# Hybrid DeltaNet, gMLP and MLP block: the operands of the MLP made ahead into device memory, one pool of 2 KB tiles, units in pairs

## The chip, the cores and the metric

The kernel runs on one core of a Trainium2 chip. The metric is the time of one execution on the device in microseconds (us), lower is better. The engines are named as in the profile: PE (TensorE, matrix products), DVE (VectorE), ACT (ScalarE), POOL (GpSimd) and SP (SyncE, which issues nearly all DMAs here). On-chip memory has 128 partitions; PSUM is the memory that PE writes to, in 8 banks of 128x512 fp32.

## What is computed

One trunk layer over 128 prompt tokens and 2048 latent tokens of width 1024, all in fp32:

```python
def block(x, s0, mod, ...):
    sh1, sc1, ga1, sh2, sc2, ga2 = mod
    h = rmsnorm(x, norm_mix_l) * (1.0 + sc1) + sh1
    o, s_new = mixer(h, s0, ...)      # projections, conv, DeltaNet scans both ways, gMLP, output projection
    x = x + ga1 * o
    h = rmsnorm(x, norm_ffn_l) * (1.0 + sc2) + sh2
    x = x + ga2 * (jnp.square(jax.nn.relu(h @ w_ff1_l)) @ w_ff2_l)
    return x, s_new
```

`w_ff1` is 1024 x 4096 and `w_ff2` 4096 x 1024. A last RMSNorm follows. The change concerns the last two lines: h, and the two products of the MLP.

## The kernel before

The 2176 tokens are 17 tiles of 128: tile 0 is the prompt, 1 to 16 are latent. Four phases follow each other; their instructions are written in an order of steps with due times, and a scheduler then sets the order on each engine.

**Projections** (to about 455 us): combined input projection and convolution; results go to device memory.

**Attention** (about 455 to 1283 us): the DeltaNet scan forward over the tiles, then backward (from about 924 us, tile 16 first), with gMLP and the output projection among the scan's steps. Each backward unit takes one tile of 128 tokens: loads, a preparation, a serial scan on PE, DVE and ACT, then the output projection. `h2_steps` (L801) belongs to a finished tile: it normalises the token rows, transposes and modulates them, and stores the result, transposed, in device memory (`h2_d`, profile name `h_d`). It runs for tiles 16 to 9 among the backward units (`spread(... h2_steps ...)`, behind L1275) and for tiles 8 to 0 during the first half of the MLP's first phase (`later`, L1548). A list of windows (`WINDOWS`) gives each kind of step its place relative to its unit.

**MLP up** (about 1283 to 2041 us): relu(h w_ff1) squared. fp32 accuracy is had from three fp32r matmuls per product, with operands split into a high and a low half (`mm3`, L215; L219 to L221). The product is done by a scheme with seven block products in place of eight: tokens are taken in two groups of 8 tiles (group 0: tiles 9 to 16; group 1: tiles 1 to 8), and a **unit** (`unit`, L1449) is one group by 256 of the 4096 hidden columns. It makes products 1, 5, 6, 7, 3, 2, 4 in this order, each 12 matmuls of 128x512 in PSUM, with sums and squares on DVE and ACT after most, and stores z (and two sums of z, `s1_d`, `s2_d`) to device memory. A unit's operands:

- the moving side (`hop`): seven operands per group, 16 KB per partition each. `token_steps` (L1356) makes them at the start of each group: 28 loads of 128x512 from `h2_d` (`hraw`), differences of these on DVE (L1377, L1383, L1388, L1395), a cast to the high half on ACT (L1369), and a subtraction for the low half on DVE (L1370). For group 0 these steps are interleaved with the first unit's weights; for group 1 they stand behind group 0's last unit.
- the stationary side (`wH`, `wL`): `weight_steps` (L1400) loads a unit's 1 MB of w_ff1 by two DMAs of 512 KB and makes the seven weight operands (`split4`, L1347: cast at L1352, subtraction at L1353), one unit ahead.

Group 1's units also do the prompt tile with 48 matmuls of 128x128 (`single`, L1523).

**MLP down** (about 2041 us to the end): z w_ff2 by the same scheme, now with seven products outside and the token pairs inside. For each of the products 1, 5, 6, 7, 3, 4, 2 the 16 moving tiles T (`t_load`, `t_build`, L1612 to L1621: load of a part of w_ff2 or of a sum of its parts in `t13_d`, `t2_d`, `t4_d`; ACT cast L1619, DVE L1620) are made during the product before; the sums are made by `sums_load` and `sums` (L1627 to L1650). The stationary tiles come from z: `s_load`, `s_build` (L1670 to L1686), with loads five steps and halves three steps ahead (`AHEAD = 3`). Results are kept in `ya`, `yb` and finished by `final` (L1704). Modulation rows for the second gate are computed among products 6 and 7 (`mods`, L1755).

**Pools.** Each phase has its own: `wp` (48 tiles of 128x512) and `stage` for projections and attention, closed by `wst.close()`; `f1w` (14 tiles `t`, 18 `hl`), `f1h`, `f1p` for MLP up; `f2w` (5 `traw`, 6 `sraw`, 20 `T`, 12 `s`), `f2p` for MLP down. A tile of a new pool waits until what used its place before is done.

```python
todo = [(gi, jp) for gi in range(2) for jp in range(NP)]
ops, steps = token_steps(9 * P)
w, prep = weight_steps(0, False)
interleave(steps, prep)
for n, (gi, jp) in enumerate(todo):
    main = unit(jp, c0, w, ops)
    nw, prep = weight_steps(todo[n + 1][1], ...)
    interleave(*[x for x in (main, prep, extra) if x])
    if n == NP - 1:
        ops, steps = token_steps(P)
        for st in steps:
            st()
```

Of the kernel before, what the change touches and what calls it, by code (L numbers as in the profile page):

```python
# [17 lines left out]
P = 128  # L18
# [34 lines left out]
FT = 14  # L53
FW = 18
# [7 lines left out]
def hybrid_step(  # L62
# [36 lines left out]
    h2_d = dp.tile([P, KT, NTOK], F32, name="h2_d")  # L99
# [6 lines left out]
    z_d = dp.tile([NT, P, 2, NK, P], F32, name="z_d")  # L106
    s1_d = dp.tile([8, P, NK, P], F32, name="s1_d")
    s2_d = dp.tile([8, P, NK, P], F32, name="s2_d")
    t13_d = dp.tile([NK, P, 2, 512], F32, name="t13_d")
    t2_d = dp.tile([NK, P, 512], F32, name="t2_d")  # L110
    t4_d = dp.tile([NK, P, 512], F32, name="t4_d")
# [54 lines left out]
    smp = ctx.enter_context(tc.tile_pool(name="small", bufs=4, reuse_waits="tile"))  # L166
    wst = ctx.enter_context(ExitStack())
# [11 lines left out]
    wp = wst.enter_context(tc.tile_pool(name="wp", bufs=48, reuse_waits="tile"))  # L179
    sp = wst.enter_context(tc.tile_pool(name="stage", bufs=NS))  # L180
# [620 lines left out]
    def h2_steps(t, psum, tmp, wide=w512):  # L801
# [17 lines left out]
        def trans2(half):  # L819
            def f():  # L820
                ps = psum()
                ev = tmp()
                for i in range(4):
                    T.transpose(ps[:, i * P : (i + 1) * P], u["x"][half][:, i * P : (i + 1) * P], ident)
                for i in range(4):
# [3 lines left out]
                store(out=h2_d[:, half * 4 : half * 4 + 4, t * P : (t + 1) * P],  # L829
                      in_=ev.rearrange("p (k d) -> p k d", k=4))  # L830
            return f

        return [norm2, trans2(0), trans2(1)]
# [4 lines left out]

    with ExitStack() as ph:
        pp = ph.enter_context(tc.tile_pool(name="prep", bufs=1, reuse_waits="tile"))  # L840
        hp = ph.enter_context(tc.tile_pool(name="hp", bufs=8, reuse_waits="tile"))
        dl = ph.enter_context(tc.tile_pool(name="scan", bufs=1, reuse_waits="tile"))
# [22 lines left out]
        def load_rows(src, t, d):  # L865
            gb = q32("gb", 3, pp)
            rows = src[t * 8 + d * 4 : t * 8 + d * 4 + 4, :].rearrange("a b -> (a b)").unsqueeze(0)
            load(out=gb.rearrange("p h d -> p (h d)"), in_=rows.to_broadcast([P, 512]))
            return gb
# [5 lines left out]
        def unit(t, d):  # L875
# [11 lines left out]
            def prep_loads():  # L887
# [3 lines left out]
                u["QK"] = q32("QK", 3, pp)  # L891
# [353 lines left out]

        events = []
# [25 lines left out]
        for i, u in enumerate(units):  # L1272
# [4 lines left out]
            for j, st in enumerate(u["prep"]):  # L1277
                at(i - w[0] + (j + 0.5) * (w[0] - w[1]) / n, st, "chain")
# [3 lines left out]
            if i >= NT:  # L1282
# [4 lines left out]
                if u["t"] > 8:  # L1287
                    spread(i + p3[8], i + p3[9], h2_steps(u["t"], pj, fraw), "fill")
# [20 lines left out]
        spread(p2[6], p2[7], [lambda n=n, k=k: load_wo(n, k) for n in range(2) for k in range(KT)], None)  # L1309
        hist = []  # L1310

        def emit(f, kind, lag):
# [6 lines left out]
            if pe and kind == "chain":  # L1319
# [17 lines left out]
    with ExitStack() as ph:  # L1337
        fw = ph.enter_context(tc.tile_pool(name="f1w", bufs=1, reuse_waits="tile"))
        fh = ph.enter_context(tc.tile_pool(name="f1h", bufs=1, reuse_waits="tile"))
        psq = ph.enter_context(tc.tile_pool(name="f1p", bufs=1, space=PSUM, reuse_waits="tile"))  # L1340

        def bank():
            return psq.tile([P, 512], F32, tag="f", name="f", bufs=8)

        def t512(name="t"):
            return fw.tile([P, 512], F32, tag="t", name=name, bufs=FT)

        def split4(src):

            h = fw.tile([P, 4, P], F32R, tag="hl", name="wH", bufs=FW)  # L1350
            lo = fw.tile([P, 4, P], F32R, tag="hl", name="wL", bufs=FW)
            A.copy(h, src)  # L1352
            V.tensor_tensor(out=lo, in0=src, in1=f32(h), op=ALU.subtract)  # L1353
            return h, lo

        def token_steps(c0):  # L1356

            ops, b, tt = {}, {}, {}

            def raw(n, kp):  # L1360
                kh, th = divmod(n, 2)
                r = t512("hraw")
                load(out=r, in_=h2_d[:, kh * 4 + kp, c0 + th * 512 : c0 + th * 512 + 512])
                return r

            def put(i, kp, src):
                if kp == 0:
                    ops[i] = fh.tile([P, 4, 2, 512], F32R, tag="hop", name="hop", bufs=7)
                A.copy(ops[i][:, kp, 0, :], src)  # L1369
                V.tensor_tensor(out=ops[i][:, kp, 1, :], in0=src, in1=f32(ops[i])[:, kp, 0, :], op=ALU.subtract)  # L1370

            def p1(kp):
                put(1, kp, raw(0, kp))

            def p5(kp):
                x, y = raw(1, kp), raw(0, kp)
                V.tensor_tensor(out=x, in0=x, in1=y, op=ALU.subtract)  # L1377
                tt[kp] = x
                put(5, kp, x)

            def p6(kp):
                x = raw(3, kp)
                V.tensor_tensor(out=tt[kp], in0=x, in1=tt[kp], op=ALU.subtract)  # L1383
                put(6, kp, tt[kp])

            def p7(kp):
                x, y = raw(3, kp), raw(1, kp)
                V.tensor_tensor(out=y, in0=x, in1=y, op=ALU.subtract)  # L1388
                put(7, kp, y)
                put(3, kp, x)  # L1390

            def p2(kp):
                x = raw(2, kp)
                put(2, kp, x)
# [5 lines left out]
        def weight_steps(jp, extra):  # L1400
# [10 lines left out]
            def a(i, j):  # L1411
                return r[j][:, :, i * P : i * P + P]
# [468 lines left out]
```

## Time and profile before

| what | us |
|---|---|
| median of 3 runs | 2753.39 |
| lowest and highest of them | 2744.67, 2754.87 |
| the profiled execution | 2746.23 |
| its span, first to last instruction | 2744.5 |
| PE busy in the span | 2637.6 |
| DVE, ACT, POOL busy | 1870.7, 1261.2, 232.0 |
| bytes moved by DMA | 541.04 MB, mean 197 GB/s |

How to read what follows. A row of the windows gives the stretch in us, its length, then for PE, PEld (weight loads), DVE, ACT and POOL the busy time with the number of instructions, then the granted clock of PE (1.00 is full), the mean busy share of the 16 DMA engines, and GB/s. A row of the groups gives line, engine, operation, out<-in, shapes and count, then busy us and mean ns, then the idle time of the engine before these instructions with what ended it. A row of the waits gives engine, line, what ended the wait, then us in total, number of times, and the longest. A row of the timeline gives start, duration, instruction, and in brackets the idle time before it. A row of the chain of waits gives start, duration and what ran. A matmul's recorded duration is longer than its share of PE's time, since matmuls overlap; the pace is read from the distance of starts.

### The profile page before, as it was taken

What the parts mean: (1) busy time and instruction counts of PE and PEld (TensorE: products, weight loads), DVE (VectorE), ACT (ScalarE), POOL (GpSimd) and SP (SyncE); (2) the same over time, 40 slices, a digit from 0 to 9 for tenths busy, and PEclk for the clock granted to TensorE, in tenths of its full rate; (3) what the DMA queues carried; (4) which work ended last, traced back from release to release, by engine and by line L of the source; (5) the groups of instructions that cost most, each with busy time, mean ns of one, the idle gap of its engine ahead of it and who ended that gap; (6) DMA issues with size and microseconds to landing.
All of it is one profiled execution on the core that took longest, in us unless ns stands there. A gap on an engine that the chain in (4) does not pass through costs nothing.

```text
span 2744.5 us, 45073 instructions
## 1 busy us (share of the span) xinstructions
PE 2637.6 (96%) x15698; PEld 2196.1 (80%) x15698; DVE 1870.7 (68%) x3911; ACT 1261.2 (46%) x3094; POOL 232.0 (8%) x448
## 2 busy tenths in 40 slices
PE   8999998999999899998899989999989999899998
PEld 4999997888887777786688877888877878688887
DVE  5867656867777887775877678566645546775675
ACT  4655555555555666642544434333323332332442
POOL 3112113111111111100000000000000000000000
PEclk9999998999999999998999999999999999999999
DMA  8867549545455667743556564443349888766664
GB/s 293 278 196 220 179 141 285 179 151 161 156 157 182 209 208 219 226 154 128 167 163 179 161 189 150 117 121 112 111 146 402 313 286 282 248 222 213 219 218 143
DMA packets 489130, 541.04 MB, mean 197 GB/s; under 512 B 32748, under 2 KB 327068, under 8 KB 488902
## 3 DMA queue, kind: packets, MB, share of 16 engines
q1 hardware_dynamic: 487894, 536.33, 61.2%
q8 instruction: 123, 2.02, 0.3%
q10 hardware_dynamic: 1008, 1.84, 0.2%
q14 instruction: 105, 0.86, 0.1%
HBM read 383.46 MB, written 154.57 MB: 196 GB/s over the span
## 4 chain that ended last, share of the span: by engine, by line
PE 78%; DMA 10%; DVE 8%; ACT 2%; issue 1%; SPq 1%; POOL 0%; DVEq 0%; POOLq 0%; ACTq 0%
PE f L220 8%; PE f L219 7%; PE f L221 7%; PE yps L220 7%; PE yps L219 7%; PE yps L221 7%; PE pj L219 6%; PE pj L221 6%; PE pj L220 6%; PE pd L885 2%; DMA qT<-qT_d 2%; PE pm L219 1%; PE pm L221 1%; PE pm L220 1%; DMA raw<-in_w_mod_dram 1%
## 5 line engine op out<-in xcount | busy, mean ns | idle before, releaser
L219 PE MATMUL yps<-T,zH 128*128 128x512 f32 x960 | 373.6, 394 | 15.9 <-ACT T L1619 15.7
L220 PE MATMUL yps<-T,zH 128*128 128x512 f32 x960 | 377.0, 393 | 5.4 <-DVE T L1620 5.3
L219 PE MATMUL f<-hop,wH 128*128 128x512 f32 x896 | 355.9, 399 | 22.4 <-ACT hop L1369 9.6
L221 PE MATMUL yps<-T,zL 128*128 128x512 f32 x960 | 375.4, 392 | 0.0
L220 PE MATMUL f<-hop,wH 128*128 128x512 f32 x896 | 354.6, 396 | 11.1 <-DVE hop L1370 10.9
L221 PE MATMUL f<-hop,wL 128*128 128x512 f32 x896 | 353.1, 395 | 0.0
L1684 ACT CAST zH<-sraw 128x512 fp32r<-128x512 f32 x240 | 147.2, 622 | 287.6 <-PE yps L220 223.4
L219 PEld LDWEIGHTS yps<-T,zH 128*128 128x128 f32 x960 | 181.9, 190 | 59.7 <-ACT T L1619 18.9
L219 PEld LDWEIGHTS f<-hop,wH 128*128 128x128 f32 x896 | 170.8, 191 | 62.8 <-ACT hop L1369 13.2
L220 PEld LDWEIGHTS yps<-T,zH 128*128 128x128 f32 x960 | 181.8, 189 | 48.4 <-DVE T L1620 10.4
L1685 DVE TENSOR_TENSOR zL<-sraw,zH 128x512 fp32r<-128x512 f32 x240 | 163.2, 687 | 80.4 <-ACT zH L1684 71.4
L220 PEld LDWEIGHTS f<-hop,wH 128*128 128x128 f32 x896 | 170.5, 190 | 53.3 <-DVE hop L1370 19.7
L221 PEld LDWEIGHTS yps<-T,zL 128*128 128x128 f32 x960 | 181.8, 189 | 37.3
L221 PEld LDWEIGHTS f<-hop,wL 128*128 128x128 f32 x896 | 170.5, 190 | 35.1 <-DVE wL L1353 0.2
L219 PE MATMUL pj<-kH,wH 128*128 128x386 f32 (+2 forms) x568 | 190.5, 338 | 0.3 <-DVE kH L468 0.3
L221 PE MATMUL pj<-kH,wL 128*128 128x386 f32 (+2 forms) x568 | 190.3, 335 | 0.0
L220 PE MATMUL pj<-kL,wH 128*128 128x386 f32 (+2 forms) x568 | 189.4, 334 | 0.0
L177 POOL TENSOR_TENSOR r<-rsq,nhalf 128x1 f32<-128x1 f32 (+1 forms) x38 | 26.7, 701 | 1593.6 <-DVE rsq L176 1593.6
L1352 ACT CAST wH<-raw 128x512 fp32r<-128x512 f32 x112 | 69.5, 622 | 139.8 <-PE f L220 138.9
L518 DVE SCALAR_TENSOR_TENSOR cv<-pj,vec,cv 128x384 f32<-128x384 f32 (+2 forms) x164 | 87.4, 540 | 58.4 <-ACT cv L515 57.2
L1352 ACT CAST wH<-s 128x512 fp32r<-128x512 f32 x96 | 59.9, 624 | 132.1 <-PE f L220 112.4
L1353 DVE TENSOR_TENSOR wL<-raw,wH 128x512 fp32r<-128x512 f32 x112 | 77.2, 691 | 52.0 <-ACT wH L1352 40.8
(402 smaller groups left out, 6185.9 us busy)
## 6 DMA issues: line engine op xcount, KB each, us to landing
sraw<-z_d SPq DMA_DIRECT2D x209, 256.0 KB
raw<-in_w_ff_dram SPq DMA_DIRECT2D x64, 512.0 KB
z_d<-c SPq DMA_DIRECT2D x96, 256.0 KB
sraw<-s_d SPq DMA_DIRECT2D x96, 256.0 KB
raw<-in_w_mod_dram SPq DMA_DIRECT2D x80, 256.0 KB
s_d<-s SPq DMA_DIRECT2D x64, 256.0 KB
traw<-t_d SPq DMA_DIRECT2D x64, 256.0 KB
hraw<-h_d SPq DMA_DIRECT2D x56, 256.0 KB
```

The source lines that it names most:

```text
L177: G.tensor_tensor(out=out, in0=t[:np_, :n], in1=nhalf[:np_, :n], op=ALU.pow)
L219: T.matmul(ps, lh, rh, start=first and i == 0, stop=False, skip_group_check=more)
L220: T.matmul(ps, lh, rl, start=False, stop=False, skip_group_check=more)
L221: T.matmul(ps, ll, rh, start=False, stop=last and i == n - 1, skip_group_check=more)
L518: V.scalar_tensor_tensor(out=cv[:, o : o + m], in0=ps[:, s + sh : s + sh + m], scalar=convw[:, w, j : j + 1], in1=cv[:, o : o + m], op0=AL ...
L885: T.matmul(p[:, h, :], lhs[:, h, :], rhs[:, h, :], start=True, stop=True)
L1352: A.copy(h, src)
L1353: V.tensor_tensor(out=lo, in0=src, in1=f32(h), op=ALU.subtract)
L1684: A.copy(h, r)
L1685: V.tensor_tensor(out=lo, in0=r, in1=f32(h), op=ALU.subtract)
```

## The change

- **Operands made ahead.** For tiles 9 to 12 and 1 to 4, `h2_steps` no longer stores `h2_d`. It loads the stored `h2_d` of the partner tile (`t + 4`), makes the part of each of the seven operands that belongs to the two tiles, both halves, and stores it to `hop_d[group, operand]` in device memory (`put`). For tiles 9 to 12 these steps run in attention, over the stretch of one unit behind the tile's own steps; for tiles 4 to 1 they run in group 0 of MLP up (`later`). `hop_next` loads one operand, 2 MB, with two DMAs; operands 1 and 5 of group 0 are loaded after the last preparation of a scan unit, the other five at the start of the MLP, those of group 1 after the products of group 0's last unit. `token_steps` is gone.
- **One pool.** `wp`, now 49 tiles of 2 KB per partition, stays open to the end and serves weights, raw tiles, z, results and rows in all phases. Seven tiles of 16 KB (`hopA` 2, `hopB` 5) hold the operands of MLP up, then the T tiles and the kept results x and q of MLP down. `hopA` takes the place of the pool `prep`, closed early (`swap_right`).
- **Units in pairs where operands change.** Units 0 and 1, 14 and 15 of each group alternate product by product, so that each moving operand serves two products in a row. Weights are made 6 products ahead (`LEAD`), their loads issued 10 products ahead. The weights' loads are four DMAs of 256 KB in place of two of 512 KB. The prompt tile's matmuls are spread over the unit's products.
- **First tiles of MLP down** (T of product 1 and the first z tiles) are made during the last 16 products of MLP up.
- **Device tensors split**: `h2_d` per tile, `z_d` in 5, `s1_d` and `s2_d` in 2, the sums of w_ff2 one tensor per product and part (`t_d`).

Per engine, the orders of the two kernels have as many PE instructions before as after; the DMA issues on SP go from 2028 to 2235.

The core of the diff:

```diff
-                store(out=h2_d[:, half * 4 : half * 4 + 4, t * P : (t + 1) * P],
-                      in_=ev.rearrange("p (k d) -> p k d", k=4))
+                if t in h2_d:
+                    store(out=h2_d[t][:, half * 4 : half * 4 + 4, :], in_=ev.rearrange("p (k d) -> p k d", k=4))
+                else:
+                    u[half] = ev
...
+        def partner():
+            u["y"] = [wide("y"), wide("y")]
+            for half, y in enumerate(u["y"]):
+                load(out=y.rearrange("p (k d) -> p k d", k=4), in_=h2_d[t + 4][:, half * 4 : half * 4 + 4, :])
+
+        def put(o, src):
+            dst = hop_d[t <= 8, o][:, :, :, (t - 1) % 4 * P : (t - 1) % 4 * P + P]
+            h = wp.tile([P, 512], F32R, tag="w", name="opH")
+            lo = wp.tile([P, 512], F32R, tag="w", name="opL")
+            A.copy(h, src)
+            V.tensor_tensor(out=lo, in0=src, in1=f32(h), op=ALU.subtract)
+            for i, part in enumerate((h, lo)):
+                store(out=dst[:, :, i, :], in_=f32(part).rearrange("p (k d) -> p k d", k=4))
+
+        def plain():
+            put(1, u[0])
+            put(2, u[1])
+        def third():
+            put(3, u["y"][1])
+            d = wide("d")
+            sub(u["y"][1], u["y"][0], d)
+            put(7, d)
+        def fifth():
+            sub(u["y"][0], u[0])
+            put(5, u["y"][0])
+        def sixth():
+            sub(u["y"][1], u["y"][0])
+            put(6, u["y"][1])
+        def fourth():
+            sub(u[1], u["y"][1])
+            put(4, u[1])
+
+        ops = [] if t in h2_d else [partner, plain, third, fifth, sixth, fourth]
+        return [norm2, trans2(0), trans2(1)] + ops
...
+    def hop_next():
+        g, o = hop_order.pop(0)
+        hop[g, o] = t = hop_tile(F32R, o in ORDER[:2])
+        for k in range(0, 4, 2):
+            load(out=f32(t)[:, k : k + 2], in_=hop_d[g, o][:, k : k + 2])
...
-                    spread(i + p3[8], i + p3[9], h2_steps(u["t"], pj, fraw), "fill")
+                    st = h2_steps(u["t"], pj, fraw)
+                    spread(i + p3[8], i + p3[9], st[:3], "fill")
+                    spread(i + p3[9], i + p3[9] + 1, st[3:], None)
...
+        tend = max(e[0] for e in events if e[3] == "prep")
+        at(tend + 0.01, swap_right)
+        for j in range(2):
+            at(tend + 0.02 + j, lambda: hop_next())
...
+    blocks = [[0, 1]] + [[n] for n in range(2, NP - 2)] + [[NP - 2, NP - 1], [NP, NP + 1]]
+    blocks += [[n] for n in range(NP + 2, 2 * NP - 2)] + [[2 * NP - 2, 2 * NP - 1]]
+    for b in blocks:
+        order = ORDER if b[0] < NP else ORDER[:-1] + (0, 4)
+        seq += [(o, n, b) for o in order for n in b]
...
+    for p in range(LEAD):
+        if p < 5:
+            hop_next()
+        weights_at(p)
+    for p, (o, n, b) in enumerate(seq):
+        u = units[n]
+        loads_at(p + LEAD + 4)
+        weights_at(p + LEAD)
+        while later and later[0][0] <= p:
+            later.pop(0)[1]()
...
+        if o:
+            u.step(o)
...
+        if n == NP - 1:
+            hop_next()
+        e = p - last
+        if e >= 0 and e % 2:
+            if e // 2 == 0:
+                for m in range(AHEAD):
+                    s_next(m, True)
+                t_ahead(0, 4)
+            elif e // 2 < 5:
+                for k in range(4 * (e // 2) - 4, 4 * (e // 2)):
+                    t_next(0, k)
```

786 lines of the change are left out of this document (370 added, 416 removed).

## The prediction

> **What bounds the kernel now.** I read the head of the page first, then busy time by windows, then TensorE's waits and the timeline at the longest of them.
>
> ```profile
> PE 2637.6 (96%) x15698; PEld 2196.1 (80%) x15698; DVE 1870.7 (68%) x3911; ACT 1261.2 (46%) x3094; POOL 232.0 (8%) x448
> ...
> PEclk9999998999999999998999999999999999999999
> ```
>
> TensorE (PE) is busy in 96% of the span, and the change neither adds nor takes a matmul: the orders of the two kernels have equally many PE instructions. What can go is only time in which PE stands or runs at a lower clock, and it lies in few places. The windows, with PE, PEld, DVE, ACT, POOL, granted clock, DMA share and GB/s:
>
> ```profile
> 1283.00:1375.00 92.00, 70.62 (x260) 51.57 (x259) 72.06 (x123) 46.17 (x90) 4.88 (x2) 0.83 0.61 195
> 1350.00:1630.00 280.00, 276.50 (x1246) 227.53 (x1245) 197.60 (x331) 131.20 (x267) 6.39 (x8) 1.00 0.55 162
> 1632.00:1660.00 28.00, 16.82 (x67) 10.96 (x65) 21.15 (x34) 13.42 (x24) 0.00 (x0) 0.88 0.93 328
> 1680.00:2025.00 345.00, 345.00 (x1861) 297.90 (x1860) 211.66 (x327) 114.17 (x199) 0.00 (x0) 1.00 0.39 115
> 2041.20:2080.00 38.80, 24.46 (x88) 18.62 (x88) 21.05 (x33) 13.04 (x24) 0.00 (x0) 0.78 1.00 374
> 2075.00:2245.00 170.00, 170.00 (x752) 140.66 (x751) 83.97 (x131) 61.68 (x109) 0.00 (x0) 1.00 0.92 325
> 2246.00:2256.00 10.00, 9.27 (x38) 6.46 (x36) 7.53 (x12) 4.50 (x8) 0.00 (x0) 1.00 0.95 341
> 2334.00:2370.00 36.00, 28.18 (x93) 18.42 (x92) 28.68 (x47) 11.80 (x21) 0.00 (x0) 0.86 0.80 265
> 2380.00:2730.00 350.00, 350.00 (x1546) 289.82 (x1545) 238.97 (x399) 123.45 (x237) 9.12 (x16) 1.00 0.64 209
> ```
>
> The last row is the undisturbed pace: 350 / 1546 = 0.2264 us per 128x512 matmul. What a window lost is its length less its matmuls at that pace. Start of the MLP: 92 - 260 x 0.2264 = 33.1. Switch of groups: 28 - 67 x 0.2264 = 12.8. From MLP up to MLP down: 38.8 - 88 x 0.2264 = 18.9. Two changes of product in MLP down: 1.4 and 14.9, so 16.3. Together 81 us. The rows between them (1350, 1680, 2075) lose nothing: VectorE at 71%, or DMA at 92%, holds nobody up there. What ended the waits:
>
> ```profile
> PE pd L971 <- DVE P L962: 17.0, 27, 2.1
> PE yps L219 <- ACT T L1619: 15.7, 5, 11.6
> PE f L220 <- DVE hop L1370: 10.9, 13, 1.7
> PE f L219 <- ACT hop L1369: 9.6, 5, 7.2
> PE f L219 <- ACT wH L1352: 8.5, 1, 8.5
> PE yps L220 <- DVE T L1620: 5.3, 10, 1.8
> ```
>
> All but the first wait for operands of the MLP: hop (made from the normalised tokens, L1369/L1370), wH (weights) and T (moving side of MLP down). The lowered clock comes on top, in the clock column: 0.78 at the entry to MLP down, 0.83 at the start of the MLP. The first row is the scan's own chain, which stays.
>
> **The change part by part.** The sum is made against the profiled execution, 2746.23 us (span 2744.5 and 1.7 around it); the median of the three runs is 7.2 us above it, the fastest 1.6 below.
>
> Part 1, start of the MLP. The units of what leaves:
>
> ```profile
> 1291.84 0.79 PE L219 MATMUL f<-hop,wH 128*128 128x512 f32 x1 [8.55 <-ACT wH L1352]
> ...
> L1370 DVE TENSOR_TENSOR hop<-hraw,hop 128x512 fp32r<-128x512 f32 x28 | 18.5, 697 | 5.7 <-ACT hop L1369 5.7
> ...
> L1388 DVE TENSOR_TENSOR hraw<-hraw 128x512 f32<-128x512 f32 x4 | 2.8, 696 | 0.0
> ...
> L1369 ACT CAST hop<-hraw 128x512 fp32r<-128x512 f32 x28 | 16.2, 620 | 24.6 <-DMA hraw<-h_d 19.6 <-DVE hraw L1383 3.0 <-DVE hraw L1388 1.2
> ```
>
> Today 28 loads, 28 casts, 28 subtractions and 16 differences stand between the last block of attention and the first seven products: 44 VectorE instructions, 44 x 0.697 = 31 us of DVE, with the weights' halves beside them. Afterwards seven operands of 2.1 MB come by DMA, the first two before attention ends. Two units share each operand, so one is wanted every 24 x 0.2264 = 5.4 us; at the 374 GB/s of the full row above its load takes 2.1 / 0.374 = 5.6 us. The five later operands thus keep pace only just, while the first units' weights share the queue. What is late next is operand six or the weights of the second product, whose casts in the changed order stand behind the last casts of attention on ACT. I leave 6 of 33 us: **-27** (from -33, nothing lost, to -15, every later operand 3 to 4 us late).
>
> Part 2, switch of groups. The operand of group 1 is loaded into the tile that unit 15's product has just released, twelve products (12 x 2.72 = 33 us) before its use, against 5.6 us for the load. The second group's 31 us of DVE are gone from there. **-12** (-13 to -8).
>
> Part 3, entry to MLP down. One pool serves both phases, so the first T and z tiles no longer wait for the old pools to be released; they are made during the last 16 products, where by the row of 1680 DMA stands at 0.39, DVE at 211.66/345 = 0.61. **-18** (-19 to -12).
>
> Part 4, changes of product within MLP down. Most loss is at 2334, where these ended the waits:
>
> ```profile
> DVE sraw L1681 <- DMA sraw<-z_d: 17.3, 8, 4.8
> ACT T L1619 <- DMA traw<-t_d: 16.3, 4, 10.5
> ```
>
> Both are landings. Raw tiles come from a pool of 49 in place of 6 and 5, and each part of t_d is a tensor of its own, so that a load waits only for its own store; but loads are issued no further ahead (4 tiles, AHEAD 3) and the bytes are the same. I take half: **-8** (from -16 to +10; the upper end if loads for z are now queued behind those for T). The Trainium skill, page "DMA: Bandwidth & Descriptors", section "Where 436 GB/s comes from", has device-memory transfers bound at about 358 GB/s per core: by that the 325 of the row at 2075 is nearly full, and this part would be worth 0. The row of 2041 with 374 disagrees, and I go by the row.
>
> Part 5, what is paid. The operands are now made in attention (tiles 12 to 9) and in group 0 of the MLP (tiles 4 to 1). Per tile: 7 casts on ACT, 7 subtractions and 4 differences on DVE, 14 stores and 2 loads of 262 KB on SP, less two stores of h2_d. By the rows of part 1 that is 11 x 0.697 = 7.7 us of DVE, 7 x 0.620 = 4.3 us of ACT and a net 3.67 MB. The stores have runs of 512 B. What such runs take is read from the row of 1680, where MLP up moves nearly only these: 115 / 0.39 = 295 GB/s at full share. A tile costs 3.67 / 0.295 = 12.4 us of DMA, four cost 50. The place:
>
> ```profile
> 900.00:950.00 50.00, 42.35 (x380) 34.92 (x380) 45.83 (x127) 30.63 (x91) 7.43 (x10) 0.97 0.71 230
> ...
> 1081.00:1175.00 94.00, 90.10 (x778) 73.02 (x777) 73.33 (x195) 63.04 (x197) 17.70 (x21) 1.00 0.71 221
> 1175.00:1283.00 108.00, 107.82 (x808) 88.90 (x806) 63.94 (x162) 38.12 (x125) 5.05 (x5) 1.00 0.33 105
> ```
>
> The four backward units of these tiles take about the 94 us of the second row. DVE has 94 - 73.3 = 20.7 us free there and gets 31: 10 too many. DMA has 0.29 x 94 = 27 us free and gets 50: 23 too many. The third row has room for a backlog (0.67 x 108 = 72 us of DMA), but scan operands queue behind it, and the scan cannot run ahead without them. The first row is the nearest case of a nearly full VectorE (92%): PE lost 7.65 of 50 us. Also, 34 of 49 tiles hold output weights and gate rows until attention's end, so 15 serve the puts, and a tile wants 21: by the order with its waits, later casts and subtractions wait for the landing of a store issued shortly before, and the scan's copies on ACT and DVE stand behind them. I take **+25**, nearest to the DMA overload; bounds +5 (all hidden in the room of the third row) and +60 (below). The Trainium skill, the same page, "Specifications", has line rate from 512 B up: by that the stores would take 14.7 / 0.374 = 39 us and this part about +14; the row of 1680 speaks against it.
>
> In group 0 the same 31 us of DVE and 50 of DMA fall on the last 64 products, 64 x 2.72 = 174 us. From the row of 1350, DVE goes from 0.71 to 0.71 + 31/174 = 0.88, DMA from 0.55 to 0.55 + 50/174 = 0.84. Weights are made six products (16 us) ahead, which covers most waits: **+4** (0 to +20).
>
> Hidden and costed at nothing: the smaller w_ff1 loads (four of 256 KB in place of two of 512 KB, 207 more issues on SP, whose queue isn't on the path in those stages), pool sides, and phase 1 and forward scan, whose order stays within +-3 us.
>
> Sum: -27 - 12 - 18 - 8 + 25 + 4 = -36; 2746.2 - 36 = **2710 us**.
>
> **The rivals.**
>
> A, attention absorbs the puts. For it: the room of 72 us behind them; PE at 107.8 of 108 there. Against: DVE beyond full in the four units. All gaps close, at their best: -33 - 13 - 19 - 16 + 5 = -76, 2670.
>
> B, the start's stall moves: operands and weights come late at the start, part 1 gives only -5. For it: 5.6 us a load against 5.4 wanted. Against: two operands are there early. 2710 + 22 = 2732.
>
> C, attention pays what the start gained: +60 in place of +25, 2745. For it: DVE and DMA both overfull, in the same four units. It needs 15 us per tile.
>
> D, the slower side: each tile's puts block ACT and DVE until earlier stores have landed. A landing from this chain is
>
> ```profile
> 1286.67 6.60 DMA hraw<-h_d
> ...
> 1354.99 5.39 DMA x<-x_d
> ```
>
> about 6 us. In the changed order the last tile's seven casts stand in a row on ACT with four such waits; 4 x 6 = 24 us per tile if nothing runs ahead, 96 for four: -65 + 4 + 96 = +35, 2781. It is slower by 0.5% once the four tiles lose over 82 us, 20.5 each. Against: the steps are spread over more than one unit for the other three tiles, and stores wait only while the slots are out.
>
> **How the numbers follow.** Forecast (2690 to 2738) 0.37; A 0.19; B 0.09; C 0.16; D 0.19. The predicted time is the forecast's 2710. A measurement of this kernel can tell about 0.5% from no change, so 2739.6 to 2767.2 counts as the same: faster 0.37 + 0.19 + 0.09 = 0.65, same 0.16, slower 0.19. The range must reach into A and D: 2664 to 2778 leaves out some 0.04 below and, above, about half of D, 0.10.
>
> **What would show it.** Parts 1 to 3: in the windows after attention's end, at the switch and at the entry to MLP down, length less matmuls at 0.2264 falls to about 6, 1 and 1 us, the waits for hop L1369/L1370 are gone, and the clock stays near 1. Part 4: the row around the changes of product loses about 8. Part 5: the backward units of tiles 12 to 9 get longer by about 6 us each, with DVE and DMA shares above 0.9, and casts of opH waiting for store landings; group 0 loses under 5 us. I am wrong if attention grows by over 60 us or not at all, or if one of the three gaps stays.

## The result and the profile after

The changed kernel takes 2792.8 us (median of 4 runs, 2787.39 to 2800.44) against 2754.13 us before (4 runs, 2744.67 to 2756.36): a ratio of 1.0149, 95% interval 1.0115 to 1.0183. It is slower by 39 us; the forecast was 2710 and the range 2664 to 2778. The profiled execution of the changed kernel is the slowest of the four, 2800.44 us.

The head of its page, to be read against that of before: PE has as many instructions and is busy 18 us longer.

```profile
PE 2655.7 (95%) x15698; PEld 2209.5 (79%) x15698; DVE 1869.1 (67%) x3909; ACT 1246.6 (45%) x3092; POOL 232.7 (8%) x448
...
PEclk9999999999999999899999898999999999999999
DMA  8866649555455667884758667433459997876682
```

A slice is 70 us long here. The clock's digit is 8 in three slices: 1119 to 1189 us (the backward units with the new steps), 1539 to 1609 (group 0 of MLP up) and 1679 to 1749 (the switch of groups). Where the time went is seen best by the starts of the matmul of the same number in PE's order. Both kernels have equally many PE instructions in each phase; near a border two of the same number need not do the same work.

| matmul | before, us | after, us | after less before | gained or lost since the row above |
|---|---|---|---|---|
| last of attention | 1282.9 | 1319.7 | +36.8 | +36.8 |
| early in group 0 | 1353.1 | 1360.9 | +7.7 | -29.1 |
| near the end of group 0 | 1623.1 | 1691.1 | +68.1 | **+60.4** |
| some 25 us into group 1 | 1667.4 | 1742.8 | +75.3 | +7.2 |
| near the end of MLP up | 2033.0 | 2106.8 | +73.8 | -1.5 |
| some 25 us into MLP down | 2080.8 | 2137.3 | +56.5 | -17.3 |
| last of all | 2735.5 | 2789.6 | +54.2 | -2.3 |

The windows of the changed kernel that stand against those of before (columns as there): start of the MLP, group 0, the 31 us up to the switch of groups, group 1, entry to MLP down, and an undisturbed stretch of MLP down.

```profile
1320.00:1358.00 38.00, 38.00 (x168) 31.16 (x167) 13.54 (x21) 8.81 (x17) 0.00 (x0) 1.00 0.91 338
1361.00:1691.00 330.00, 281.59 (x1200) 228.00 (x1201) 216.12 (x359) 141.66 (x296) 6.45 (x8) 0.92 0.67 198
1691.00:1722.00 31.00, 12.72 (x50) 10.10 (x49) 8.17 (x14) 3.76 (x7) 0.00 (x0) 0.72 0.75 289
1740.00:2100.00 360.00, 360.00 (x1915) 308.19 (x1915) 223.88 (x356) 121.03 (x223) 0.00 (x0) 1.00 0.42 123
2105.00:2125.00 20.00, 20.00 (x116) 17.34 (x115) 7.28 (x11) 3.41 (x7) 0.00 (x0) 1.00 0.71 196
2440.00:2590.00 150.00, 150.00 (x655) 122.80 (x654) 95.13 (x151) 46.99 (x79) 0.00 (x0) 1.00 0.70 226
```

Three things are to be seen. The start of the MLP and the entry to MLP down have no gap left: PE is busy in all 38 and all 20 us. Group 0 lost 330 - 1200 x 0.2264 = 58 us, with PE idle in 48 of them, although VectorE is busy in only 65% and DMA in 67%: neither of the two that the prediction had watched is full there. And the last row has 655 matmuls in 150 us, 0.2290 us each, with PE busy throughout and the clock at 1.00; before it was 0.2264. What ended PE's waits in group 0 (1319 to 1725), then two of ACT's waits in the same stretch:

```profile
PE f L217 <- ACT x L1491: 21.6, 2, 15.1
PE f L217 <- ACT p L1502: 21.1, 2, 18.3
PE f L822 <- DVE x L815: 16.4, 3, 8.4
PE f L217 <- ACT p L1495: 10.0, 2, 8.6
```

```profile
ACT junk L811 <- DMA x<-x_d: 46.7, 13, 11.4
ACT x0H L1421 <- DMA x<-h_d: 36.1, 2, 21.1
```

L1491, L1495 and L1502 are ACT's copies of results out of PSUM; L822 are the transposes of `h2_steps`, which wait for the rows that L815 has normalised. L811 is the square in `norm2`, which stands in the code right behind the load of its rows; x0H is the cast of the prompt tile's operand, right behind its load.

### The profile page after: what moved, and what is told of

It is laid out like the page before. It is cut to its first block, busy times and chain, and to the rows that moved or that the text cites. A ratio compares the mean times of both kernels' runs of the same rounds, so it can differ in the third digit from the quotient of the medians.

```text
span 2798.7 us, 45208 instructions
## 1 busy us (share of the span) xinstructions
PE 2655.7 (95%) x15698; PEld 2209.5 (79%) x15698; DVE 1869.1 (67%) x3909; ACT 1246.6 (45%) x3092; POOL 232.7 (8%) x448
## 4 chain that ended last, share of the span: by engine, by line
PE 75%; DMA 10%; DVE 9%; issue 2%; ACT 2%; SPq 1%; POOL 1%; DVEq 0%; POOLq 0%; ACTq 0%
PE f L217 14%; PE f L219 14%; PE f L218 14%; PE pj L217 6%; PE pj L219 5%; PE pj L218 5%; PE pd L943 2%; DMA x<-x_d 2%; DMA qT<-qT_d 2%; PE pm L217 1%; PE pm L219 1%; PE pm L218 1%; PE pd L1120 1%; PE pt L568 1%; PE pd L1121 1%
## 5 line engine op out<-in xcount | busy, mean ns | idle before, releaser
L219 PE MATMUL f<-hop,zL 128*128 128x512 f32 x960 | 377.0, 393 | 1.8 <-DVE zL L1415 1.8
L217 PE MATMUL f<-hop,zH 128*128 128x512 f32 x960 | 376.7, 393 | 1.9 <-ACT zH L1421 1.9
L218 PE MATMUL f<-hop,zH 128*128 128x512 f32 x960 | 377.0, 393 | 0.0
L1421 ACT CAST zH<-zraw 128x512 fp32r<-128x512 f32 x240 | 147.0, 620 | 292.6 <-DVE zraw L1415 85.8
L217 PEld LDWEIGHTS f<-hop,zH 128*128 128x128 f32 x960 | 180.4, 188 | 45.5 <-ACT zH L1421 2.7
L219 PEld LDWEIGHTS f<-hop,zL 128*128 128x128 f32 x960 | 180.3, 188 | 44.9 <-DVE zL L1415 2.6
L218 PEld LDWEIGHTS f<-hop,zH 128*128 128x128 f32 x960 | 180.2, 188 | 40.9
L1415 DVE TENSOR_TENSOR zL<-zraw,zH 128x512 fp32r<-128x512 f32 x240 | 162.8, 687 | 70.8 <-ACT zH L1421 54.2
L217 PEld LDWEIGHTS pj<-kH,wH 128*128 128x128 f32 x568 | 107.2, 189 | 4.9 <-issue 4.4
L217 PE MATMUL pj<-wH,hH 128*128 128x512 f32 x248 | 110.4, 445 | 0.0
```

What stands on the lines that cost most here:

```text
L217: T.matmul(ps, lh, rh, start=first and i == 0, stop=False, skip_group_check=more)
L218: T.matmul(ps, lh, rl, start=False, stop=False, skip_group_check=more)
L219: T.matmul(ps, ll, rh, start=False, stop=last and i == n - 1, skip_group_check=more)
L1415: V.tensor_tensor(out=out, in0=a, in1=b, op=op)
```

## The experiments

"Group 0" below is the time from the first matmul of MLP up to the first of group 1, read from the starts on PE's timeline: 349.5 us before, 402.1 in the changed kernel. "Attention's end" is the start of its last matmul: 1282.9 before, 1319.7 in the changed kernel's profile. The theories were: the loads of group 0 come late and the engines' orders pass the wait on (**late loads**); the puts' own work fills VectorE and DMA (**work of the puts**); the address of the moving tiles sets the pace of matmuls (**address**).

**a1_align.** One tile of 32 bytes ahead on the right side.

```diff
+    edge = ctx.enter_context(tc.tile_pool(name="edge", bufs=1, side="right"))
+    pad = edge.tile([P, 8], F32, tag="pad", name="pad")
```

> The changed kernel with one 32-byte tile ahead on the right side of the memory, so that the two hopA tiles (and the scan's pool before them) begin at a multiple of 64 bytes (196544 in place of 196576). In the profile of the changed kernel each matmul whose moving side lies in hopA is followed after 0.2336 us on average, the others after 0.2267. Theory 'address': the offset of 32 bytes does this; then the row of the undisturbed stretch of MLP down gives 0.2267 us per matmul again, MLP down loses some 8 us and the second group of MLP up some 5, 13 to 15 us in all, with the stalls of group 0 left as they are. Theory 'place' (the upper part of the memory, or contention with DMA, is slower whatever the offset): nothing changes, 0.231 stays.

Measured: 2782.4 us (one run; before took 2743.39 on the same chip). In MLP down two of every five groups of four T tiles lie in hopA (`hop_tile`). Matmuls on these are followed after 0.2297 us on average (pauses left out), in the changed kernel after 0.2340, with 0.2267 as the undisturbed pace; MLP down took 669.1 us from its first matmul to its last, 673.2 in the changed kernel. The window of MLP down in a1:

```profile
2440.00:2580.00 140.00, 140.00 (x614) 114.93 (x613) 87.60 (x138) 45.17 (x77) 0.00 (x0) 1.00 0.71 227
```

140 / 614 = 0.2280, somewhat over half of the way back. The address matters, but a multiple of 64 bytes is not enough. Group 0 stayed at 399.9.

**a2_early_loads.** The loads of `norm2` in MLP up as a step of their own, six products ahead; the prompt tile's operand loaded six products ahead of its cast.

```diff
+        def get():
+            u["x"] = [wide("x"), wide("x")]
+            for n in range(2):
+                load(out=u["x"][n], in_=x2_d[t * P : (t + 1) * P, n * 512 : (n + 1) * 512])
...
+    later = [e for e in later] + [(later[j][0] - 6, -1, get) for j, get in gets]
...
+        if p == half - 14:
+            first_raws = first_load()
```

> The changed kernel with the loads of h2_steps in MLP up issued six products (16 us) ahead of their use, and those of the prompt tile's operands 6 products ahead; all else, puts included, the same. Theory 'late loads' (ACT and PE wait in their order for x_d and h_d loads that are issued only just before, which in group 0 is 68 us of loss over before): waits of ACT on x_d (46.7 us) and on the prompt tile's h_d (36.1) go, and group 0 gets 25 to 45 us shorter. Theory 'work of the puts' (VectorE and DMA are too full in group 0): under 10 us gained, the waits move to other instructions.

Measured: 2723.39 us, with 2743.39 for before on the same chip. Group 0 took 336.0 us, 66 less than in the changed kernel's profile and 62 to 64 less than in a1 and a4, more than the theory asked for. ACT's waits on x_d and h_d are gone. PE's waits in group 0 of a2:

```profile
PE f L217 <- ACT x L1497: 9.1, 2, 8.6
PE f L828 <- DVE x L821: 4.5, 2, 2.8
PE f L217 <- ACT p L1508: 0.4, 1, 0.4
```

All puts are still there. The load on VectorE was no obstacle: in a2's window of the same stretch it is busy in 207.05 of 265 us, 78%.

```profile
1349.00:1614.00 265.00, 250.93 (x1103) 203.50 (x1102) 207.05 (x347) 134.73 (x283) 6.94 (x8) 0.97 0.74 216
```

**a3_no_puts_g0.** The six steps of the operands do nothing for tiles 4 to 1.

```diff
+        if t <= 8 and ops:
+            ops = [lambda: None] * 6
...
-            load(out=f32(t)[:, k : k + 2], in_=hop_d[g, o][:, k : k + 2])
+            load(out=f32(t)[:, k : k + 2], in_=hop_d[0, o][:, k : k + 2])
```

> The changed kernel without the operands of tiles 1 to 4: their steps in group 0 do nothing (28 casts, 44 VectorE operations, 56 stores and 8 loads left out; the steps of the normalisation keep their places), and group 1 loads group 0's operands, so half of the result is of other numbers. Theory 'work of the puts': nearly all of the 68 us that group 0 lost goes. Theory 'late loads': the stalls at the start of group 0 (21.6 us by matmul 9600) stay, and with them waits on x_d; 15 to 35 us gained.

Measured: 2761.59 us; group 0 took 375.4, 23 to 27 less than with the puts. 39 us more than in a2 are left with no put at all. So the late loads lose time by themselves and the puts deepen it. Where the loads are early, the puts cost little: apart from the 9.1 us at the start, PE waits 4.9 us in a2.

**a4_raw_first.** Unit 2's weights loaded ahead of the five operands.

```diff
         if p < 5:
             hop_next()
+        if p == 1:
+            loads_at(14)
```

> The changed kernel with the four loads of unit 2's weights issued before the five operands of group 0 and not behind them, in SP's order. In the profile of the changed kernel SP issues ten loads of 1 MB, then the weights' loads until 1349, the cast of the weights waits 9.9 us for them, and from there TensorE loses 21.6 us in group 0's first 60 us before any put. Theory 'lead lost at the start': these 20 us go, and the later stalls get smaller too, 20 to 45 us in all, against some 4 us that the operands come later. Theory 'each stall for itself' : only the 10 us of the first wait go. If the puts' work is all, nothing is gained.

Measured: 2788.56 us, group 0 398.5. Nothing is gained; the lead of the weights at the start is not what group 0 loses by.

**b0_early_align.** a2 with a pad of 96 bytes, so that hopA begins at 196480, a multiple of 128 (the cut shows a1's pad against this one).

```diff
-    pad = edge.tile([P, 8], F32, tag="pad", name="pad")
+    pad = edge.tile([P, 24], F32, tag="pad", name="pad")
```

> The changed kernel with the loads of h2_steps issued early (as in a2) and the right side of the memory moved to a multiple of 128 bytes (hopA at 196480). a2 gave 2723 beside 2743 of before on its chip, and a1 with a multiple of 64 only brought matmuls on hopA from 0.2336 to 0.2290 us. Theory 'address, 128 bytes': 0.2267 on hopA, so that the gains add, 10 to 14 us below a2, that is 30 to 35 us below before. Theory 'address, 64 bytes is all that counts, the rest is the place': 0.2290 stays, 5 to 8 us below a2. Ratio to before 0.987 to 0.990 by the first, 0.990 to 0.993 by the second.

Measured: 2711.57 us (4 runs), ratio to before 0.9869, interval 0.9843 to 0.9894. Matmuls on hopA are followed after 0.2269 us on average, and MLP down takes 663.7 us, 9.5 less than in the changed kernel; a2, with the same early loads and the old address, took 673.7. Its window, beside that of the changed kernel above (0.2290 us per matmul) with 150 / 663 = 0.2262:

```profile
2430.00:2580.00 150.00, 150.00 (x663) 124.25 (x662) 104.61 (x173) 55.61 (x105) 3.65 (x5) 1.00 0.71 232
```

**b9_before_shift.** The other way round: the kernel before, with 32 bytes ahead of the pool of `hop`.

```diff
+        edge = ph.enter_context(tc.tile_pool(name="edge", bufs=1))
+        pad = edge.tile([P, 8], F32, tag="pad", name="pad")
...
         fh = ph.enter_context(tc.tile_pool(name="f1h", bufs=1, reuse_waits="tile"))
```

> The kernel before with a 32-byte tile ahead of the pool of hop in MLP up, so that all seven moving operands begin 32 bytes behind a multiple of 128 (98720 in place of 98688) and nothing else moves but x0. Theory 'address': matmuls on hop are followed after 0.2336 us in place of 0.2267, 2688 of them, so MLP up takes 15 to 18 us longer. Theory 'place' or 'pool': no change within 3 us.

Measured: 2755.53 us (one run; before 2746.39, median of 7). MLP up took 761.4 us from its first matmul to its last, 749.1 before: 12.3 more, somewhat under the 15 to 18. Matmuls on the shifted operands are followed after 0.2332 us on average, 0.2273 before. The address is shown as the cause, in both directions; nothing else moves here but the prompt tile's operand.

**c1_no_puts_att.** b0 without the puts of tiles 9 to 12.

```diff
+        if t > 8 and ops:
+            ops = [lambda: None] * 6
```

> b0 without the operands of tiles 9 to 12 in attention (28 casts, 44 VectorE operations, 56 stores and 8 loads left out; the seven loads of group 0's operands read another tensor of the same size, so half of the result is of other numbers). If the puts are what attention pays, its last matmul falls back to within 5 us of before's 1283 on the same kind of chip, from 1309; if part of it is the order of the steps or the pools' new places, 5 to 15 us over before remain.

Measured: 2686.32 us; attention's end at 1284.6, against 1307.4 in b0 and 1282.9 before. The puts cost attention 23 us; all the rest of the change is worth under 2. The stretch of those four units, b0 first, then c1:

```profile
1080.00:1185.00 105.00, 87.65 (x753) 71.51 (x748) 90.09 (x220) 71.16 (x216) 19.69 (x22) 0.94 0.85 267
```

```profile
1080.00:1185.00 105.00, 99.83 (x873) 81.06 (x872) 83.94 (x222) 67.27 (x210) 20.20 (x24) 1.00 0.64 209
```

120 matmuls fewer in b0's 105 us, VectorE at 86%, the clock at 0.94.

**c3_spread.** b0 with the steps of tiles 12 to 9 drawn out.

```diff
-                    spread(i + p3[8], i + p3[9], st[:3], "fill")
-                    spread(i + p3[9], i + p3[9] + 1, st[3:], None)
+                    t0 = i + p3[8] + 0.75 * max(0, 12 - u["t"])
+                    spread(t0, t0 + p3[9] - p3[8], st[:3], "fill")
+                    spread(t0 + p3[9] - p3[8], t0 + 1.75, st[3:], None)
```

> b0 with the steps of tiles 12 to 9 in attention drawn out: each tile's normalisation and operands begin 0.75 units later per tile, and the operands take about 1.2 units, so that they reach into the units of tiles 4 to 2, where DMA stood at 33% and VectorE at 59% in the profile of before. In the changed kernel attention ended 26 us (a1, a3, a4) to 37 us later than in before. Theory 'overfull stretch' (VectorE and DMA over their room in four units): 10 to 20 us of that come back. Theory 'slots' (each put waits for the landing of a store, with 15 tiles): little comes back, as the tiles hold their slots longer, 0 to 8 us, or it gets worse by up to 10.

Measured: 2698.14 us (4 runs), ratio 0.9819, interval 0.979 to 0.9849. Attention's end at 1296.3: 11 of the 23 us come back. With this the change beats the kernel before by 1.8%.

**e1_raw_first.** c3 with a4's edit.

> c3 with unit 2's four weight loads issued ahead of the five operands, the edit that brought nothing in a4. In c3 one gap of 9.05 us is left at the start of the MLP (1338 to 1347, PE waits for ACT's copy behind the weights' cast). Theory 'lead lost at the start, hidden in a4 by the later waits': 7 to 10 us now, ratio to before 0.976 to 0.980. Theory 'the operands are what is late': nothing, or up to 3 us worse, as the operands now come 3 us later; ratio 0.981 to 0.983.

Measured: 2696.6 us (5 runs), ratio 0.9819, interval 0.9799 to 0.9839: no difference from c3. The gap at the start is still there, 8.44 us from one start to the next (1337.8 to 1346.3). A miss. ACT's longest wait in this stretch was 11.3 us for unit 2's weights in c3, and is 9.8 us for rows x_d here. The wait moved to the next load that stands behind the operands.

**b1_x_only.** a2 with the prompt tile's operand loaded late again.

> The changed kernel with the early loads of h2_steps alone; the prompt tile's operands are loaded just before their use as in the changed kernel. From the start of the MLP to the second group's first matmul the changed kernel took 402 us (398 to 400 in a1 and a4), a2 336. The longest single gap, 18.7 us, stood before the prompt tile's cast. If the two kinds of late load each bear their part, 350 to 360; if one late load is enough to lose the lead for all, over 370; if the prompt tile's was no cause, 336 to 340.

Measured: 2731.01 us; group 0 took 343.2, a2 336.0. So the loads of the normalisation bear nearly all of it, and the prompt tile's load 7 us; it lost 18.7 only where the rest was late too. None of the three answers fits well; the third is nearest.

**h1_small_stores.** b0 with the bytes of the puts' stores cut in attention.

```diff
+                if t > 8:
+                    store(out=dst[:, 0, i, 0:32], in_=f32(part)[:, 0:32])
```

> b0 with the 56 stores of the operands in attention cut to 128 x 128 bytes each (all casts, VectorE operations and issues stay, and the waits of a put for the landing of an earlier store; the operands of group 0 are read from another tensor, so half of the result is of other numbers). Attention ended at 1307 in b0 and at 1285 without the puts (c1). Theory 'DMA overfull': 1287 to 1293. Theory 'VectorE and ACT overfull': 1300 to 1307. In between, both.

Measured: 2704.4 us; attention's end at 1302.8, 4.5 earlier than in b0. Eight executions with the same puts end attention between 1306.4 and 1319.7, so 4.5 is within their scatter. What is lost against before from the matmul at 1093 on scatters less: 22.2 to 24.6 us in seven of them (27.1 in the profile of the changed kernel), 16.8 here, 0.6 in c1. The bytes are worth 4.5 to 6 of 23 us.

**d3_stores_only.** b0 without casts and subtractions of the puts in attention; the source is stored twice.

```diff
+            if t > 8:
+                for i in range(2):
+                    store(out=dst[:, :, i, :], in_=src.rearrange("p (k d) -> p k d", k=4))
+                return
```

> b0 with the 28 casts and 28 subtractions of the puts in attention left out; the differences stay, and the source is stored twice, so all 56 stores with their bytes stay (the operands of group 0 are not split, so the result is less exact). No tile waits for a put's landing then. Attention ended at 1307 in b0, 1303 with small stores, 1285 without the puts. Theory 'work on VectorE and ACT, and the slots that it waits for': 1287 to 1293. Theory 'the issue and the bytes': 1298 to 1305.

Measured: 2696.69 us; attention's end at 1295.9. Casts, halves and the slots that they wait for are worth some 11 of the 23 us (11.5 by the end, 10.8 by the growth from 1093), the bytes 4.5 to 6; the rest, 6 to 7, is left to issues, differences and loads, or to their acting together. The result lies between the two theories.

**g1_no_pairs.** c3 with all units one by one.

```diff
-    blocks = [[0, 1]] + [[n] for n in range(2, NP - 2)] + [[NP - 2, NP - 1], [NP, NP + 1]]
-    blocks += [[n] for n in range(NP + 2, 2 * NP - 2)] + [[2 * NP - 2, 2 * NP - 1]]
+    blocks = [[n] for n in range(2 * NP)]
```

> c3 with all units one by one, the operands loaded as before. A new operand is then wanted every 2.72 us where it takes 5.6 us to load. Theory 'pairs pay at the start': the first 40 us of the MLP lose 10 to 16 us more than in c3, the switch of groups nothing (there the tiles come free one unit, 19 us, ahead): 10 to 16 us in all. If the loads are early enough anyway, under 3 us.

Measured: 2701.94 us (one run), group 0 335.5 against 333.6 in c3. Pairs are worth 2 to 4 us, not 10 to 16: two gaps, of 3.2 us early and of 3.7 later, take the place of c3's single gap of 9.05.

**d1_trans_later.** The changed kernel, late loads as they are, but the next tile's normalisation put ahead of a tile's transposes.

```diff
+    per = [h2_steps(t, bank, lambda: w512("junk"), w512) for t in range(8, -1, -1)]
+    later = [per[0][0]]
+    for a, b in zip(per, per[1:] + [[]]):
+        later += b[:1] + a[1:]
```

> The changed kernel, late loads and puts as they are, but in group 0 each tile's transposes come at least four steps (19 us) behind its normalisation, in place of one (4.8 us), by putting the next tile's normalisation ahead of them. Group 0 with the switch took 399 to 402 us in the changed kernel and 336 with early loads. Theory 'PE waits in its order for the transposes' input': 340 to 360. Theory 'ACT waits in its order for the load, weights' casts and copies behind it': over 380. Waits of PE on the normalised rows (16.4 us in three) go in both.

Measured: 2746.01 us; group 0 took 356.7, of which 17.8 are the one gap before the prompt tile's operand. ACT still waits for the loads, as long as in the changed kernel; PE does not wait for the rows:

```profile
ACT junk L811 <- DMA x<-x_d: 44.3, 12, 7.7
...
ACT x0H L1421 <- DMA x<-h_d: 35.3, 2, 20.4
```

```profile
PE f L217 <- ACT p L1502: 17.4, 1, 17.4
PE f L217 <- ACT x L1491: 7.5, 2, 4.9
PE f L217 <- ACT ev L825: 4.1, 1, 4.1
PE f L822 <- DVE x L815: 2.5, 2, 2.3
```

So the place of the transposes costs: they stand in PE's order before their input is there. ACT's 44 us of waiting for x_d cost little by themselves. Apart from the prompt tile's gap, group 0 takes 339 us here, near a2's 336.

**e2_pool_queue.** c3 with the five later operands of group 0 issued by GpSimd.

```diff
-            hop_next()
+            hop_next(G.dma_start)
```

> c3 with the ten loads of group 0's last five operands issued by GpSimd and not by SP, so that they do not stand behind the last x_d stores there, nor unit 3's weights behind them. In c3 they were issued from 1299 to 1308 and a gap of 9.05 us followed at 1338. Theory 'order on SP': the gap goes, 6 to 10 us less, ratio to before 0.978 to 0.980. Theory 'bytes': 10 MB take 28 us whoever issues them, the gap stays within 3 us, ratio 0.981 to 0.983.

Measured: 2700.26 us (4 runs), ratio 0.9829, interval 0.9805 to 0.9853; the gap at the start is 8.40 us. Issuing them elsewhere brings nothing (c3: 2698.14). The Trainium skill, page "DMA: Bandwidth & Descriptors", section "Issuing engines are not separate DMA queues", says that all issuers share the same 16 DMA engines and that only issue time is saved; this run agrees.

**f2_spread_more.** c3 with 0.9 units and 2.0 units in place of 0.75 and 1.75.

> c3 with each tile's steps beginning 0.9 units later per tile and not 0.75, and lasting 2.0 units and not 1.75, so that the last end at the unit of tile 1. c3 ended attention at 1296, without the puts it is 1285. If the overfull stretch is what is left: 1290 to 1294, 2 to 6 us less in all. If the last steps now come too late for the first operands' loads: the first matmul of the MLP waits, and the time is above c3's.

Measured: 2706.38 us (4 runs), ratio 0.9859, interval 0.9834 to 0.9884; attention's end at 1305.8, 9.5 later than in c3. Worse, and by neither of the two ways expected: attention itself ends later, and the first matmul of the MLP follows its last after 0.2 us. Where those 9.5 us go was not followed further.

## Why the prediction was wrong, step by step

**Part 1, start of the MLP: right.** -27 forecast, -29.1 in the profile. The window at 1320 has no gap. The reason given for it, pairs that give a load 5.4 us, carries little of it: without pairs the gain is 2 to 4 us less (g1).

**Part 2, switch of groups: the step right, its neighbour missed.** The operands of group 1 are there, and the wait for hop is gone; but the prompt tile's operand, loaded just before its cast, got into the queue among them:

```profile
1691.47 0.43 SPq L1554 DMA_DIRECT2D x<-h_d  x1
1692.00 5.57 SPq L893 DMA_DIRECT2D hop<-hop_d  x6
1697.63 0.41 SPq L1554 DMA_DIRECT2D x<-h_d  x1
```

```profile
1715.03 0.80 PE L217 MATMUL f<-hop,wH 128*128 128x512 f32 x1 [18.28 <-ACT p L1502]
```

The second of the two loads was issued behind six loads of 1 MB and its cast ran at 1713.87, 16 us later, with ACT's copies behind it. In place of -12 the profile shows +7.

**Part 3, entry to MLP down: right.** -18 forecast, -17.3 measured; PE has no gap from 2105 to 2125.

**Part 4, changes of product: right in sign, too small.** The starts of the matmuls on both sides of the two changes give -3.9 and -10.7 (after less before goes from +61.4 to +57.5 and from +59.0 to +48.3), some -15 where -8 stood. It was eaten up by what no part had: the pace on hopA, 9.5 us in MLP down (b0 against the changed kernel).

**Part 5, attention: right.** +25 forecast; the profiled execution shows 27.1 between the matmuls at 1093 and 1200 of before (+9.7 to +36.8), seven other executions with the same attention 22 to 25. The +9.7 ahead of the puts is 0.4 to 5 in those. The reasons held only in part: VectorE, ACT and slots some 11, bytes 4.5 to 6 of 23 (d3, h1). I had taken the 25 from the overload of DMA, so that the size came out is partly luck. VectorE and DMA reached 0.86 and 0.85 (b0), not the 0.9 named as a sign. Rival D put the whole loss here, at 82 us or more; that did not happen. Its mechanism, casts of opH that wait for a store to land, cost ACT 4.6 us in the profile (1090 to 1215).

**Part 5, group 0: this step failed.** It said +4 (0 to +20), from VectorE at 0.88 and DMA at 0.84, and "weights are made six products (16 us) ahead, which covers most waits". Measured: +60. Of the 90 us between the forecast and the profiled execution, 56 lie here; 19 lie in part 2, 12 in attention and 6 in MLP down, with 3 gained elsewhere. The shares stayed below the forecast (0.65 and 0.67 in group 0 of the changed kernel, 0.78 and 0.74 in a2, which loses little); the loss did not come from full engines. I counted the new steps as work and did not look at what they do to the steps already there. Before, two steps of `h2_steps` went into each unit, one per 3.5 products, 9.5 us; now 51 steps share 90 products, one per 1.76, 4.8 us. In `norm2` the load stands directly ahead of its use, and the transposes are the next step. A load of 256 KB took 4 to 7 us to land (4.1 and 4.3 for x_d in this kernel's chain of waits, 5.4 and 6.6 in the two rows that the prediction shows), and then come the square, the scale and the product. At 9.5 us that is enough: the kernel before has the same late load, and PE waits for the rows (L824 there) hardly at all.

```profile
PE f L824 <- DVE x L817: 0.3, 1, 0.3
```

At 4.8 us it is not: PE waits 16.4 us at the transposes (L822 above). Then ACT's copies and casts behind their evacuation come late, so do VectorE's results, and on SP the next loads stand behind stores that wait for these results. The prediction had put SP's queue down as off the path. One round of it in the changed kernel, behind a first wait of 2.35 us at the transposes, up to 1360.9; SP, ACT, then PE:

```profile
1371.60 1.00 SPq L809 DMA_DIRECT2D x<-x_d  x1
1373.54 0.36 SPq L1481 DMA_DIRECT2D z_d<-c  x1
1373.99 0.46 SPq L809 DMA_DIRECT2D x<-x_d  x1
1379.66 0.36 SPq L1481 DMA_DIRECT2D z_d<-c  x1
```

```profile
1376.77 0.63 ACT L811 ACTIVATE junk<-x 128x512 f32<-128x512 f32 x1 [5.36 <-DMA x<-x_d]
...
1378.11 0.63 ACT L811 ACTIVATE junk<-x 128x512 f32<-128x512 f32 x1 [0.62 <-DMA x<-x_d]
...
1379.25 0.57 ACT L1491 COPY x<-f 128x512 f32<-128x512 f32 x1
```

```profile
1379.88 0.79 PE L217 MATMUL f<-hop,wH 128*128 128x512 f32 x1 [15.11 <-ACT x L1491]
```

The load is issued at 1371.6, its square runs at 1376.8, the copy that PE waits for comes behind it at 1379.3, and PE goes on at 1379.9 after 15 us. PE's wait here is for ACT, and 6.0 of its 15.1 us are ACT's own two waits for the loads (5.36 and 0.62); the second load was issued 2.4 us behind the first, after a store of z. In d1 ACT waits as long in all, but apart from the prompt tile's gap PE never waits over 4.9 us. That late loads are the cause is shown (a2, b1), and that they cost by way of transposes close behind them is shown (d1). That the added steps bring it about by their spacing is supported by the kernel before and by a3, where the spacing stays and the puts' work is gone, and 39 us are still lost; the old spacing was not tried with the puts. The way round through SP is read from the timeline and was not tried by itself.

**The rivals.** A, B and C did not come. The sign was D's, the place and the mechanism were not. "Slower" had 0.19.

**Still open:** the gap of 8 to 9 us that c3 keeps 40 us into the MLP. It stayed with unit 2's weights first (e1) and with the operands issued elsewhere (e2); it went to two of 3 to 4 us without pairs. That 10 MB of operands simply take that long, so that whatever load stands next is late, fits ACT's waits in c3 and e1, but is argued, not shown.

## What to carry to other kernels

When steps are added to a sequence that is spread over a fixed stretch, look at what the closer spacing does to the steps already there: a load directly ahead of its use is covered only by the distance to the next step that needs it. With VectorE at 65% and DMA at 67%, 60 us were still lost in a stretch, since each wait was passed on along the order of the other engines; a load moved to a place of its own brought all of it back, with the added work still there. And when pools are moved, compare the starting addresses of the matmul operands with those of before.

## What the runs showed of the hardware

**The address of the moving tile sets the pace of matmuls.** Where each 128x512 fp32r tile began at a multiple of 128 bytes, the next matmul started after 0.2269 us (b0); 64 bytes past such a multiple, after 0.2297 (a1); 96 bytes past, after 0.2340 on average (most between 0.231 and 0.238, the changed kernel); 32 bytes past, 0.2332 (b9). Other offsets were not tried. It showed in the changed kernel (hopA at 196576), went in two steps (a1 at 196544, b0 at 196480), and could be brought into the kernel before (b9). It appears neither as a wait nor in the clock, only as fewer matmuls per window. The Trainium skill, page "SBUF — State Buffer", section "Operand start alignment", asks for a start at a multiple of the element's size. All four addresses keep to that; these runs add what the address costs in time.

**Device memory.** The second group's operands came in at up to 447 GB/s; the DMA view of the changed kernel from 1640 to 1715, GB/s in 40 slices:

```profile
GB/s 303 317 309 299 236 190 0 0 0 0 91 49 0 133 248 183 162 354 385 391 395 424 419 341 297 376 359 300 367 389 447 424 419 419 424 419 419 416 189 2
```

The Trainium skill, page "DMA: Bandwidth & Descriptors", section "Where 436 GB/s comes from", gives about 358 GB/s for transfers between device memory and the core; here loads of 1 MB in 8 KB runs hold 416 to 447 for a fifth of the window, and the measurement decides.
